# Two input chunks side by side, bias tiles and residual spread over one transfer queue, in a two-layer encoder trunk

## Chip, cores and metric

One core of one Trainium2 chip. The metric is the device time of one execution in microseconds (us). TensorE (PE) multiplies; VectorE (DVE) and ScalarE (ACT) prepare operands and do the elementwise work; GpSimd (POOL) and SyncE (SP) issue transfers, POOL with a little arithmetic. Each engine runs its own instructions in the order of a list that is fixed when the kernel is built; engines wait for each other through semaphores.

## The reference, cut

S = 256 tokens of width D = 2048, two layers. Only layer 0's attention and the bias table matter here.

```python
h = rms_norm(x, norm_attn[i])
proj = h @ w_in_a[j]                       # 2048 x 5120
q, k, v, q_m = jnp.split(proj, [MIX_WIDTH, 2 * MIX_WIDTH, 3 * MIX_WIDTH], axis=-1)   # MIX_WIDTH = 1536
q = rms_norm(q.reshape(B, S, N_HEADS, 2, DIFF_QK_DIM), a_q_norm[j])    # k alike; 12 heads
...
bias = rel_bias_lookup(rel_bias, positions[:, None, :] - pb[:, :, None])   # 32 buckets x 12 heads
s = s + jnp.transpose(bias, (0, 3, 1, 2))[:, :, None].astype(jnp.float32)
p = jax.nn.softmax(s, axis=-1)
a = p[:, :, 0] - lam * p[:, :, 1]
...
x = x + heads @ w_out[i]
h = rms_norm(x, norm_mlp[i])
x = x + jnp.square(jax.nn.relu(h @ w_up[i])) @ w_down[i]
```

## The kernel before

**Weights.** Every weight matrix is cut into chunks of 512 output columns, and a chunk of the input projection into 8 *pieces* of 128x1024 f32 (512 KB: two blocks of 128 rows of the matrix). `fetch` (L171) issues a piece's transfer on SP (L183), casts it on ACT to a rounded `hi` (L184) and subtracts on DVE to get the rest, `lo` (L185). `chunk_tok` (L264) runs 12 matmuls of 128x512 for each piece into two PSUM banks called mm: per block of rows and half of the tokens hi by x (L276), lo by x (L277), hi by the rest of x (L278). raw, hi and lo have four buffers each; `piece` keeps two pieces fetched ahead. Chunks 6 to 8 of the input projection are values, 0 to 2 queries, 3 to 5 keys. The order is 6, 0, 3, 7, 1, 4 and so on; pieces are counted here in that order over chunks, so chunk 6 is pieces 0 to 7, chunk 0 pieces 8 to 15, chunk 3 pieces 16 to 23, chunk 7 pieces 24 to 31 and chunk 1 pieces 32 to 39.

**The start.** Chunk 6 runs while the input arrives. Its pieces come in halves (256 KB); ahead of each half `first` (L732) loads x tiles on ACT's queue (L724) and splits one of 16 blocks of x on ACT and DVE (L200, L201). The residual `xt` is loaded in four parts of 512 KB on SP (L730); the parts stand behind the latest weight transfer (`tc.issue_after`).

**Tasks.** Everything else is cut into tasks, and `tick` (L138), called after each piece, runs the next step of the first ready task; that sets where the step's instructions come in the program, and a scheduler then sets the order on each engine by its own estimate of times. The 8 tasks `rows_done` build the bias: `bias_hot(i)` loads 4 blocks of 32x2048 buckets, issued by POOL (L560), and compares them with each partition's number (L562, DVE); `bias_rows(i)` looks the bias up by 48 small matmuls (L571, *rows* below) into two banks called aux and copies these, the first on DVE, the second on ACT (L572). `norm_T` squares a finished q or k chunk (L324), sums (L326), takes the root (L109 to L114), scales (L331) and transposes (L339); `row_stats` and `chunk_sq` do the like for x. `diff_head` does a head's scores (12 matmuls, L386), adds the bias and takes the maximum (L392, DVE), negates it (L394) and takes the exponent (L395, ACT), later the values.

**Lanes.** The transfers that SP and ACT issue take eight completion semaphores in turn; one is issued only when the transfer eight before it has landed.

Of the kernel before, what the change touches and what calls it, by code (L numbers as in the profile page):

```python
# [31 lines left out]
BW = 14  # L32
# [14 lines left out]
def trunk(ctx: ExitStack, tc: tile.TileContext, xin, xtok, memin, pos, rel, gcol, rows,  # L47
# [113 lines left out]
    for layer, (name, chunks) in enumerate((("a", (6, 0, 3, 7, 1, 4, 8, 2, 5, 9)), ("b", (3, 4, 0, 1, 2, 5)))):  # L161
        plan_chunks(name, chunks)
        plan_chunks(f"mem{layer}", range(2))
        plan_chunks(f"out{layer}", range(4))
        plan_chunks(f"up{layer}", range(16))
        plan_down(f"down{layer}")
# [4 lines left out]
    def fetch(parts=1, lead=None):  # L171

        name, c, j = plan.popleft()
        src = weights[name][c, j]
# [3 lines left out]
        n = 1024 // parts  # L178
        for i in range(parts):
            s = slice(i * n, (i + 1) * n)  # L180
            if lead is not None:
                lead(i)
            behind[0] = nc.sync.dma_start(raw[:, s], src[:, s])  # L183
            nc.scalar.copy(hi[:, s], raw[:, s])  # L184
            nc.vector.tensor_tensor(lo[:, s], raw[:, s], as32(hi)[:, s], op=ALU.subtract)  # L185
        ready.append(((name, c, j), hi, lo))

    def piece(name, c, j, lead=None):

        if lead is not None:  # L190
            fetch(2, lead)
        else:
            while plan and len(ready) <= AHEAD:
                fetch()
        key, hi, lo = ready.popleft()
        assert key == (name, c, j), (key, name, c, j)
        return hi, lo
# [66 lines left out]
    def chunk_tok(w, c, X2, before=None, lead=None, steps=1):  # L264
        ps = [bank("mm") for _ in range(2)]
        for j in range(8):
            if before is not None:
                before(j)
            hi, lo = piece(w, c, j, lead and (lambda i: lead(2 * j + i)))
            for kk in range(2):  # L270
                for t in range(2):
                    k = 2 * j + kk
                    ws = slice(kk * 512, kk * 512 + 512)
                    xh = X2[k][:, 0, t * P:(t + 1) * P]
                    xl = X2[k][:, 1, t * P:(t + 1) * P]
                    nc.tensor.matmul(ps[t], lhsT=xh, rhs=hi[:, ws], start=(k == 0), stop=False)  # L276
                    nc.tensor.matmul(ps[t], lhsT=xh, rhs=lo[:, ws], start=False, stop=False)  # L277
                    nc.tensor.matmul(ps[t], lhsT=xl, rhs=hi[:, ws], start=False, stop=(k == KT - 1))  # L278
            tick(steps)
        return ps  # L280

# [274 lines left out]
    def bias_hot(i):  # L556
        oh = blk([P, 8, S], BF16)
        hot = oh.rearrange("p r q -> p (r q)")
        for g in range(4):
            nc.gpsimd.dma_start(hot[32 * g:32 * g + 32, :],  # L560
                                bkt[g:g + 1, i * 2048:(i + 1) * 2048].broadcast_to([32, 2048]))
# [184 lines left out]
    rows_done = [Task([lambda i=i: bias_hot(i), lambda i=i: bias_rows(i, bias)], [prep], wait=BW) for i in range(8)]  # L746
# [103 lines left out]
```

## Time and profile before

| | us |
|---|---|
| three runs | 2148.4, 2149.2, 2148.91; median 2148.91 |
| the profiled execution | 2150.42 |
| its span on the core | 2148.6 |
| PE busy in the span | 2137.6 |

The profiled execution's own time is 1.8 us over its span and 1.5 us over the median of the runs. PE has some work in 99% of the span; the start of a matmul to the start of the next one tells more than the busy time, since matmuls overlap. The granted clock is 1.00 throughout, the 2.4 GHz level.

### The profile page before, as it was taken

What the parts mean: (1) busy time and instruction counts of PE and PEld (TensorE: products, weight loads), DVE (VectorE), ACT (ScalarE), POOL (GpSimd) and SP (SyncE); (2) the same over time, 40 slices, a digit from 0 to 9 for tenths busy, and PEclk for the clock granted to TensorE, in tenths of its full rate; (3) what the DMA queues carried; (4) which work ended last, traced back from release to release, by engine and by line L of the source; (5) the groups of instructions that cost most, each with busy time, mean ns of one, the idle gap of its engine ahead of it and who ended that gap; (6) DMA issues with size and microseconds to landing.
All of it is one profiled execution on the core that took longest, in us unless ns stands there. A gap on an engine that the chain in (4) does not pass through costs nothing.

```text
span 2148.6 us, 29416 instructions
## 1 busy us (share of the span) xinstructions
PE 2137.6 (99%) x11116; PEld 1806.4 (84%) x11116; DVE 1315.6 (61%) x2067; ACT 1083.6 (50%) x1740; POOL 35.7 (2%) x61
## 2 busy tenths in 40 slices
PE   9999999999999999999999999999999999999999
PEld 7877878888888888888888888888888888888887
DVE  7667786565555555566556677655555556556554
ACT  6456675454444445555545566554444444544443
POOL 1200020000000000000000000000000000000000
PEclk9999999999999999999999999999999999999999
DMA  8865565666666666666656656566666666666654
GB/s 292 237 209 154 157 195 153 187 183 189 185 194 188 191 186 193 193 195 235 198 194 192 181 167 178 155 183 183 185 195 188 192 189 185 196 196 212 192 193 148
DMA packets 114959, 409.24 MB, mean 190 GB/s; under 512 B 13568, under 2 KB 14336, under 8 KB 114560
## 3 DMA queue, kind: packets, MB, share of 16 engines
q1 hardware_dynamic: 111840, 401.01, 60.9%
q0 software_dynamic: 1536, 4.20, 0.8%
q10 hardware_dynamic: 1440, 2.15, 0.3%
q8 instruction: 87, 1.43, 0.3%
q14 instruction: 56, 0.46, 0.1%
HBM read 401.93 MB, written 5.37 MB: 190 GB/s over the span
## 4 chain that ended last, share of the span: by engine, by line
PE 97%; DMA 1%; DVE 1%; ACT 1%; issue 0%; SPq 0%; POOL 0%; ACTq 0%; DVEq 0%; POOLq 0%
PE mm L289 11%; PE aux L289 11%; PE mm L276 9%; PE mm L277 9%; PE mm L278 9%; PE mm L293 6%; PE aux L293 6%; PE mm L680 5%; PE mm L679 5%; PE mm L678 5%; PE aux L679 5%; PE aux L680 5%; PE aux L678 5%; DMA raw<-in_w_a 1%; PE aux L368 1%; PE aux L339 1%
## 5 line engine op out<-in xcount | busy, mean ns | idle before, releaser
L185 DVE TENSOR_TENSOR lo<-raw,hi 128x1024 fp32r<-128x1024 f32 (+1 forms) x744 | 892.7, 1214 | 747.7 <-ACT hi L184 747.3
L184 ACT CAST hi<-raw 128x1024 fp32r<-128x1024 f32 (+1 forms) x744 | 764.3, 1044 | 815.2 <-PE aux L289 194.1
L276 PE MATMUL mm<-hi,x 128*128 128x512 f32 x704 | 281.3, 401 | 2.0 <-ACT hi L184 2.0
L277 PE MATMUL mm<-lo,x 128*128 128x512 f32 x704 | 276.3, 392 | 2.1 <-DVE lo L185 2.1
L278 PE MATMUL mm<-hi,x 128*128 128x512 f32 x704 | 275.9, 392 | 0.0
L289 PE MATMUL mm<-x,hi 128*128 128x512 f32 x1024 | 247.4, 391 | 0.0
L289 PE MATMUL aux<-x,hi 128*128 128x512 f32 x1024 | 246.9, 391 | 0.0
L289 PEld LDWEIGHTS mm<-x,hi 128*128 128x128 f32 x1024 | 188.2, 188 | 36.8 <-DVE xt L642 0.5
L289 PEld LDWEIGHTS aux<-x,hi 128*128 128x128 f32 x1024 | 188.2, 188 | 36.4
L679 PE MATMUL aux<-lo,h 128*128 128x512 f32 x512 | 199.5, 390 | 0.5 <-DVE lo L185 0.5
L680 PE MATMUL aux<-hi,h 128*128 128x512 f32 x512 | 199.2, 389 | 0.0
L678 PE MATMUL aux<-hi,h 128*128 128x512 f32 x512 | 199.2, 389 | 0.0
L678 PE MATMUL mm<-hi,h 128*128 128x512 f32 x512 | 199.2, 389 | 0.0
L679 PE MATMUL mm<-lo,h 128*128 128x512 f32 x512 | 199.2, 389 | 0.0
L680 PE MATMUL mm<-hi,h 128*128 128x512 f32 x512 | 199.2, 389 | 0.0
L276 PEld LDWEIGHTS mm<-hi,x 128*128 128x128 f32 x704 | 132.2, 188 | 29.1 <-ACT hi L184 3.3
L277 PEld LDWEIGHTS mm<-lo,x 128*128 128x128 f32 x704 | 132.6, 188 | 28.2 <-DVE lo L185 4.2
L278 PEld LDWEIGHTS mm<-hi,x 128*128 128x128 f32 x704 | 132.2, 188 | 27.9 <-DVE x L201 0.2
L293 PEld LDWEIGHTS mm<-x,lo 128*128 128x128 f32 x1024 | 131.4, 191 | 4.8
L293 PEld LDWEIGHTS aux<-x,lo 128*128 128x128 f32 x1024 | 131.3, 191 | 5.0
L293 PE MATMUL mm<-x,lo 128*128 128x256 f32 x1024 | 133.3, 283 | 0.0
L293 PE MATMUL aux<-x,lo 128*128 128x256 f32 x1024 | 132.8, 283 | 0.0
(166 smaller groups left out, 2114.8 us busy)
## 6 DMA issues: line engine op xcount, KB each, us to landing
raw<-in_w_up SPq DMA_DIRECT2D x256, 512.0 KB, 3.9
raw<-in_w_down SPq DMA_DIRECT2D x256, 512.0 KB, 4.2
raw<-in_w_a SPq DMA_DIRECT2D x72, 512.0 KB, 4.0
raw<-in_w_out SPq DMA_DIRECT2D x64, 512.0 KB, 3.6
raw<-in_w_b SPq DMA_DIRECT2D x48, 512.0 KB, 3.7
raw<-in_w_mem SPq DMA_DIRECT2D x32, 512.0 KB, 3.8
raw<-in_w_a SPq DMA_DIRECT2D x16, 256.0 KB, 5.7
blk<-bkt POOLq DMA_DIRECT2D x32, 128.0 KB, 8.8
```

The source lines that it names most:

```text
L184: nc.scalar.copy(hi[:, s], raw[:, s])
L185: nc.vector.tensor_tensor(lo[:, s], raw[:, s], as32(hi)[:, s], op=ALU.subtract)
L276: nc.tensor.matmul(ps[t], lhsT=xh, rhs=hi[:, ws], start=(k == 0), stop=False)
L277: nc.tensor.matmul(ps[t], lhsT=xh, rhs=lo[:, ws], start=False, stop=False)
L278: nc.tensor.matmul(ps[t], lhsT=xl, rhs=hi[:, ws], start=False, stop=(k == KT - 1))
L289: nc.tensor.matmul(ps[o], lhsT=hi[:, cols(k % 2, o)], rhs=x2.rearrange("p a s -> p (a s)"), start=(k == 0), stop=(k == 2 * nj - 1))
L293: nc.tensor.matmul(ps[o][:, 256:512], lhsT=lo[:, cols(k % 2, o)], rhs=x2[:, 0, :], start=False, stop=False)
L339: nc.tensor.transpose(out=pt[:, h * P:(h + 1) * P], in_=qn[t][:, h * P:(h + 1) * P], identity=ident)
L368: nc.tensor.transpose(out=pt[:, kt * S + qt * P:kt * S + (qt + 1) * P], in_=p_of(qt)[:, kt * P:(kt + 1) * P], identity=ident)
L678: nc.tensor.matmul(ps[n][t], lhsT=xh, rhs=hi[:, ws], start=(k == 0), stop=False)
L679: nc.tensor.matmul(ps[n][t], lhsT=xh, rhs=lo[:, ws], start=False, stop=False)
L680: nc.tensor.matmul(ps[n][t], lhsT=xl, rhs=hi[:, ws], start=False, stop=(k == 4 * KT - 1))
```

## The change

- Chunks 6 and 0 run together (`chunk_pair`): for each of 8 steps both chunks' pieces are fetched, x is split once, and 24 matmuls run, chunk 6 into mm banks and chunk 0 into aux banks. Only step 0's pieces come in halves. The program calls `tick` twice after a step.
- The x loads go to SP's queue, ahead of the weights that need them.
- The residual comes in eight parts of 256 KB, six of them in the steps.
- The bucket tiles are loaded by SP instead of POOL, behind the latest weight transfer, and `rows_done[i]` may start at tick 16 + 2i instead of 14.
- Statistics of x and the values of chunk 6 move to behind the pair (`start_stats`), and the squares of chunk 0 behind them.

The line numbers of the changed kernel: weight transfer, cast, subtraction L174 to L176, chunk matmuls L272 to L274, x loads L744 and L758, residual L750, bucket load L583, comparison L584, rows L593, copies L594, squares L346, sums L348, root L109 to L114, scaling L353, scores L408, L414, L416, L417.

```diff
-BW = 14
+BW = 16
...
+    plan.extend(("a", c, j) for j in range(8) for c in (6, 0))
...
+    def chunk_pair(w, ca, cb, X2, lead, before):
+        pa = [bank("mm") for _ in range(2)]
+        pb = [bank("aux") for _ in range(2)]
+        for j in range(8):
+            if j == 0:
+                fetch(2, lead)
+            else:
+                before(j)
+            two = [(pa, *piece(w, ca, j)), (pb, *piece(w, cb, j))] if j else [...]
+            for kk in range(2):
+                for ps, hi, lo in two:
+                    mms_tok(ps, 2 * j + kk, hi, lo, X2)
+            tick()
+            tick()
...
     def bias_hot(i):
-        for g in range(4):
-            nc.gpsimd.dma_start(hot[32 * g:32 * g + 32, :],
-                                bkt[g:g + 1, i * 2048:(i + 1) * 2048].broadcast_to([32, 2048]))
+        with tc.issue_after(behind[0].ins):
+            for g in range(4):
+                nc.sync.dma_start(hot[32 * g:32 * g + 32, :], bkt[g:g + 1, i * 2048:(i + 1) * 2048].broadcast_to([32, 2048]))
...
+    def next_x(j):
+        if j == 1:
+            load_x(1)
+        load_x(j + 1)
+        take_x(2 * j)
+        take_x(2 * j + 1)
+        if j > 1:
+            load_residual(j - 2)
...
-    rows_done = [Task([lambda i=i: bias_hot(i), lambda i=i: bias_rows(i, bias)], [prep], wait=BW) for i in range(8)]
+    rows_done = [Task([lambda i=i: bias_hot(i), lambda i=i: bias_rows(i, bias)], [prep], wait=BW + 2 * i) for i in range(8)]
...
+    pv, pq = chunk_pair("a", 6, 0, X2, first_x, next_x)
...
+    stats = Task([lambda: (load_residual(6), load_residual(7))] + [lambda c=c: chunk_sq(c) for c in range(4)] + [start_stats],
+                 gap=1, front=True)
+    qT, qd = norm_T(pq, st0, 8, gs[:, 0:1], lambda: None)
+    qd.after.append(stats)
```

How this moves instructions is seen in the order of the built kernels.

SP's queue at the start before holds half pieces (raw) only, with the x tiles on ACT's queue; xt is the residual, rw, tab and t1k are small tables:

```order
L183 DMA raw_113<-in_w_a 128x512 x2
L183 DMA raw_147<-in_w_a 128x512 x2
L183 DMA raw_176<-in_w_a 128x512 x2
L183 DMA raw_205<-in_w_a 128x512 x2
L589 DMA rw<-in_rows 128x268
L541 DMA tab<-in_rel 32x12
L183 DMA raw_247<-in_w_a 128x512 x2
L730 DMA xt<-in_xtok 128x2x512
```

Now it holds the x tiles (xs) too, and two pieces for each step:

```order
L758 DMA xs_121<-in_xin 128x256
L174 DMA raw_115<-in_w_a 128x512
L174 DMA raw_118<-in_w_a 128x512
L758 DMA xs_121<-in_xin 128x256
L174 DMA raw_115<-in_w_a 128x512
L174 DMA raw_118<-in_w_a 128x512
L744 DMA xs_166<-in_xin 128x512
L744 DMA xs_168<-in_xin 128x512
L174 DMA raw_176<-in_w_a 128x1024
L174 DMA raw_182<-in_w_a 128x1024
```

The x loads moved from ACT's queue to SP's, ahead of the weights.

DVE before, in chunk 3: blk_602 is the bucket tile whose rows stand before piece 19, with aux_751 the first of its banks; lo_805, lo_875 and lo_945 belong to pieces 21, 22 and 23:

```order
L331 TENSOR_TENSOR t2k_635<-mm_376,sm_617 128x512
L562 TENSOR_SCALAR blk_602<-blk_602,itf 128x2048
L572 COPY big_110<-aux_681 128x12x4x8
L185 TENSOR_TENSOR lo_805<-raw_803,hi_804 128x1024
L572 COPY big_110<-aux_751 128x12x4x8
L185 TENSOR_TENSOR lo_875<-raw_873,hi_874 128x1024
L562 TENSOR_SCALAR blk_608<-blk_608,itf 128x2048
L572 COPY big_110<-aux_821 128x12x4x8
L185 TENSOR_TENSOR lo_945<-raw_943,hi_944 128x1024
```

DVE now, in the same chunk: blk_603 and blk_705 are the bucket tiles whose rows stand before pieces 20 and 22, aux_733 and aux_840 their first banks; lo_611, lo_685, lo_713 and lo_787 belong to pieces 20, 21, 22 and 23:

```order
L353 TENSOR_TENSOR t2k_909<-aux_113,sm_893 128x512
L353 TENSOR_TENSOR t2k_911<-aux_114,sm_893 128x512
L584 TENSOR_SCALAR blk_603<-blk_603,itf 128x2048
L594 COPY big_110<-aux_733 128x12x4x8
L176 TENSOR_TENSOR lo_611<-raw_609,hi_610 128x1024
L176 TENSOR_TENSOR lo_685<-raw_683,hi_684 128x1024
L584 TENSOR_SCALAR blk_705<-blk_705,itf 128x2048
L594 COPY big_110<-aux_840 128x12x4x8
L176 TENSOR_TENSOR lo_713<-raw_711,hi_712 128x1024
L176 TENSOR_TENSOR lo_787<-raw_785,hi_786 128x1024
L348 TENSOR_REDUCE sm_939<-t2k_941 128x8
L584 TENSOR_SCALAR blk_816<-blk_816,itf 128x2048
```

Before, a copy of the rows ahead of piece 19 stands between the lo of pieces 21 and 22; now the copy of the rows ahead of piece 22 stands before the lo of piece 22 itself, and the comparison of the tile for piece 24 behind a sum of chunk 3's squares.

PE now, at piece 22 (its hi is hi_712): the last of the 48 rows, then the piece's first matmuls:

```order
L593 MATMUL aux_866<-tab_453,blk_705 128x48
L272 MATMUL mm_559<-hi_712,x_464 128x512
L272 MATMUL mm_560<-hi_712,x_464 128x512
L273 MATMUL mm_559<-lo_713,x_464 128x512
L274 MATMUL mm_559<-hi_712,x_464 128x512
```

Two matmuls with hi stand between the rows and the first that needs lo. The rows stand before pieces 18 (partly 19), 20, 22, 24, 26, 28, 30 and 32 now, and before pieces 18, 19, 20, 21 (towards its end), 25, 26, 27 and 31 in the kernel before.

DVE now, ahead of piece 36: its lo, lo_1442, stands behind seven of the L414 (ISA with two outputs) of the first two heads, whose scores, with the third head's, stand on PE in one row of 36 matmuls ahead of the piece:

```order
L414 ISA t2k_1556,sm_1539<-aux_1542,big_110 128x256
L414 ISA sm_1539 128x1
L416 TENSOR_SCALAR sm_1491<-sm_1490 128x1
L414 ISA t2k_1556,sm_1539<-aux_1543,big_110 128x256
L414 ISA sm_1539 128x1
L416 TENSOR_SCALAR sm_1540<-sm_1539 128x1
L414 ISA t2k_1563,sm_1539<-aux_1542,big_110 128x256
L414 ISA sm_1539 128x1
L176 TENSOR_TENSOR lo_1442<-raw_1440,hi_1441 128x1024
```

Before, three heads' scores stand one head ahead of each of pieces 33, 34 and 35. From about piece 70 on, the two orders are the same.

## Rows read from the trace of the kernel before

**Rows 1.** The page's first part: busy time, share of the span and instructions of each engine.

```profile
PE 2137.6 (99%) x11116; PEld 1806.4 (84%) x11116; DVE 1315.6 (61%) x2067; ACT 1083.6 (50%) x1740; POOL 35.7 (2%) x61
```

**Rows 2.** Busy time by stretches of 10 us from the start: engines' busy us (instructions), then the granted clock, the DMA engines' busy share and GB/s.

```profile
0.00:10.00 10.00, 8.27 (x43) 6.95 (x44) 2.98 (x11) 3.45 (x6) 1.14 (x10) 1.00 0.77 264
10.00:20.00 10.00, 8.84 (x37) 6.36 (x36) 6.97 (x16) 5.80 (x13) 0.00 (x0) 1.00 0.99 318
20.00:30.00 10.00, 7.78 (x32) 5.43 (x31) 7.67 (x16) 7.67 (x16) 1.19 (x2) 1.00 0.85 262
```

**Rows 3.** Timeline of PE from the first matmul of chunk 6 (6.17) over chunk 0's first (34.53) to chunk 3's first (56.29): start, duration, then line, operation and, in brackets, the idle time before and what ended it. Some matmul records are missing from the trace.

```profile
6.17 0.50 PE L276 MATMUL mm<-hi,x 128*128 128x512 f32 x1
...
8.57 0.74 PE L276 MATMUL mm<-hi,x 128*128 128x512 f32 x2 [0.67 <-ACT hi L184]
...
15.41 0.50 PE L277 MATMUL mm<-lo,x 128*128 128x512 f32 x1 [0.61 <-DVE lo L185]
15.75 0.40 PE L278 MATMUL mm<-hi,x 128*128 128x512 f32 x1
...
21.45 0.73 PE L276 MATMUL mm<-hi,x 128*128 128x512 f32 x2 [0.76 <-ACT hi L184]
...
26.67 0.50 PE L277 MATMUL mm<-lo,x 128*128 128x512 f32 x1 [1.46 <-DVE lo L185]
...
34.53 0.39 PE L276 MATMUL mm<-hi,x 128*128 128x512 f32 x1
...
56.29 0.39 PE L276 MATMUL mm<-hi,x 128*128 128x512 f32 x1
```

**Rows 4.** Timeline of ACT around 20 us; ACTq is the issue of a transfer.

```profile
20.00 0.34 ACTq L724 DMA_DIRECT2D xs<-in_xin  x1
20.38 0.51 ACT L200 ACTIVATE x<-xs,gc 128x256 fp32r<-128x256 f32 x1 [4.21 <-DMA xt<-in_xtok]
```

**Rows 5.** Timeline of PE in chunk 3 at the rows of two bucket tiles.

```profile
61.74 1.38 PE L571 MATMUL aux<-tab,blk 128*128 128x48 bf16 x48
62.96 0.48 PE L276 MATMUL mm<-hi,x 128*128 128x512 f32 x1
63.28 0.40 PE L277 MATMUL mm<-lo,x 128*128 128x512 f32 x1
63.51 0.39 PE L278 MATMUL mm<-hi,x 128*128 128x512 f32 x1
...
69.83 1.38 PE L571 MATMUL aux<-tab,blk 128*128 128x48 bf16 x48
```

**Rows 6.** Timeline of DVE from the end of chunk 0 into chunk 3.

```profile
56.45 0.69 DVE L326 TENSOR_REDUCE sm<-t2k 128x8 f32<-128x512 f32 x1 [0.36 <-ACT t2k L324]
57.05 0.74 DVE L562 TENSOR_SCALAR blk<-blk,itf 128x2048 bf16<-128x2048 bf16 x1
...
59.57 0.22 DVE L327 TENSOR_SCALAR sm<-sm,st 128x8 f32<-128x8 f32 x1
...
62.64 0.17 DVE L112 TENSOR_TENSOR sm<-sm 128x16 f32<-128x16 f32 x1
...
63.26 1.29 DVE L331 TENSOR_TENSOR t2k<-mm,sm 128x512 f32<-128x512 f32 x2
64.46 0.75 DVE L562 TENSOR_SCALAR blk<-blk,itf 128x2048 bf16<-128x2048 bf16 x1
65.12 0.55 DVE L572 COPY big<-aux 128x384 f32<-128x384 f32 x1
65.59 1.22 DVE L185 TENSOR_TENSOR lo<-raw,hi 128x1024 fp32r<-128x1024 f32 x1
...
70.65 0.56 DVE L572 COPY big<-aux 128x384 f32<-128x384 f32 x1 [1.00 <-PE aux L571]
71.22 1.23 DVE L185 TENSOR_TENSOR lo<-raw,hi 128x1024 fp32r<-128x1024 f32 x1
```

**Rows 7.** Timeline of ACT in chunk 3: a cast and the two steps of a root.

```profile
60.41 1.05 ACT L184 CAST hi<-raw 128x1024 fp32r<-128x1024 f32 x1 [2.38 <-DMA raw<-in_w_a]
61.37 0.21 ACT L109 ACTIVATE sm<-sm 128x16 f32<-128x16 f32 x1
61.61 0.22 ACT L110 ACTIVATE sm<-sm 128x16 f32<-128x16 f32 x1
```

**Rows 8.** Timeline of PE, DVE and ACT around the scores of a head (three answers, one for each engine).

```profile
118.91 0.97 PE L386 MATMUL aux<-blk,blk 64*128 64x256 f32 x12
...
119.92 0.42 DVE L392 CUSTOM_DVE_ANT_0 t2k<-aux,big 128x256 f32<-128x256 f32 x1 [0.79 <-PE aux L386]
...
121.08 0.42 DVE L392 CUSTOM_DVE_ANT_0 t2k<-aux,big 128x256 f32<-128x256 f32 x1
...
121.49 1.22 DVE L185 TENSOR_TENSOR lo<-raw,hi 128x1024 fp32r<-128x1024 f32 x1
...
118.23 0.51 ACT L395 ACTIVATE t2k<-t2k,sm 128x256 f32<-128x256 f32 x1 [2.05 <-DVE sm L394]
...
118.74 0.49 ACT L395 ACTIVATE t2k<-t2k,sm 128x256 f32<-128x256 f32 x1
```

**Rows 9.** The page's last part: transfers by line, count, KB of each, median us from issue to landing.

```profile
raw<-in_w_a SPq DMA_DIRECT2D x72, 512.0 KB, 4.0
...
blk<-bkt POOLq DMA_DIRECT2D x32, 128.0 KB, 8.8
```

More of the change, by code (lines that the diff above doesn't have):

```diff
@@ L159, in plan_down @@
         plan.extend((name, c, j) for h in range(2) for j in range(32) for c in (2 * h, 2 * h + 1))
[L161 removed]
+    plan.extend(("a", c, j) for j in range(8) for c in (6, 0))
+    for layer, (name, chunks) in enumerate((("a", (3, 7, 1, 4, 8, 2, 5, 9)), ("b", (3, 4, 0, 1, 2, 5)))):
         plan_chunks(name, chunks)
@@ L169, in trunk, with fetch_part, new_piece @@
     behind = [None]
-    def fetch(parts=1, lead=None):
-        name, c, j = plan.popleft()
-        src = weights[name][c, j]
+    def fetch_part(key, raw, hi, lo, s):
+        name, c, j = key
+        behind[0] = nc.sync.dma_start(raw[:, s], weights[name][c, j][:, s])
+        nc.scalar.copy(hi[:, s], raw[:, s])
+        nc.vector.tensor_tensor(lo[:, s], raw[:, s], as32(hi)[:, s], op=ALU.subtract)
+    def new_piece():
         raw = wp.tile([P, 1024], F32, tag="raw", name=nm("raw"))
@@ L177, in fetch, with piece @@
         lo = wp.tile([P, 1024], F32R, tag="lo", name=nm("lo"))
[L178 to L181, printed above, removed]
-                lead(i)
[L183 to L194, printed above, removed]
+        return plan.popleft(), raw, hi, lo
+    def fetch(n=1, lead=None):
+        new = [new_piece() for _ in range(n)]
+        for i in range(2 if lead else 1):
+            if lead:
+                lead(i)
+            for p in new:
+                fetch_part(*p, slice(i * 512, i * 512 + 512) if lead else slice(0, 1024))
+        ready.extend((p[0], p[2], p[3]) for p in new)
+    def piece(name, c, j):
+        while plan and len(ready) <= AHEAD:
+            fetch()
         key, hi, lo = ready.popleft()
@@ L262, in to_features, with mms_tok, chunk_tok @@
         return Task([lambda: two(0), lambda: two(1)], wait=1, gap=1)
-    def chunk_tok(w, c, X2, before=None, lead=None, steps=1):
+    def mms_tok(ps, k, hi, lo, X2):
+        ws = slice((k % 2) * 512, (k % 2) * 512 + 512)
+        for t in range(2):
+            xh = X2[k][:, 0, t * P:(t + 1) * P]
+            xl = X2[k][:, 1, t * P:(t + 1) * P]
+            nc.tensor.matmul(ps[t], lhsT=xh, rhs=hi[:, ws], start=(k == 0), stop=False)
+            nc.tensor.matmul(ps[t], lhsT=xh, rhs=lo[:, ws], start=False, stop=False)
+            nc.tensor.matmul(ps[t], lhsT=xl, rhs=hi[:, ws], start=False, stop=(k == KT - 1))
+    def chunk_tok(w, c, X2, before=None, steps=1):
         ps = [bank("mm") for _ in range(2)]
@@ L268, in chunk_tok @@
                 before(j)
-            hi, lo = piece(w, c, j, lead and (lambda i: lead(2 * j + i)))
+            hi, lo = piece(w, c, j)
             for kk in range(2):
[L271 to L278, printed above, removed]
+                mms_tok(ps, 2 * j + kk, hi, lo, X2)
             tick(steps)
         return ps
+    def chunk_pair(w, ca, cb, X2, lead, before):
[6 more added lines that the diff above has]
+                before(j)
+            two = [(pa, *piece(w, ca, j)), (pb, *piece(w, cb, j))] if j else [(pa, *ready.popleft()[1:]), (pb, *ready.popleft()[1:])]
+            for kk in range(2):
+                for ps, hi, lo in two:
+                    mms_tok(ps, 2 * j + kk, hi, lo, X2)
+            tick()
+            tick()
+        return pa, pb
     def chunk_out(w, c, nj, x2_of, tag, steps=1):
```

51 lines of the change are left out of this document (22 added, 29 removed).

## The prediction

> **What bounds the kernel now.** The page's first part comes first: PE is busy 2137.6 us [rows 1], 99% of a span of 2148.6, so time can only come from the 11.0 us in which it has nothing, or go by adding to them. The stretches of 10 us show where they lie: PE works 8.27, 8.84 and 7.78 of the first three [rows 2], so 5.1 of the 11.0 us fall into the first 30 us, at the full clock. The timeline of PE is then read from start to start, because a matmul's end is modelled: chunk 6 goes from 6.17 to 34.53, 28.36 us, and chunk 0 behind it from 34.53 to 56.29, 21.76 us for the same 96 matmuls [rows 3]. Chunk 6 loses 6.60 us. In brackets stand its waits, for hi and lo in turn, with 1.46 us the longest. On ACT a wait of 4.21 us ends at 20.38 [rows 4], for a transfer of the residual: the x load issued at 20.00 stood behind a lane which that transfer held. Chunk 3 is read next, because the change moves its order: there PE goes from matmul to rows to matmul without a gap [rows 5].
>
> **Part 1: the pair.** A step of the pair is 24 matmuls, 2 x 21.76 / 8 = 5.44 us, and needs one step of x, where before a piece of 2.72 us needed it. ACT's work in a step is two casts of 1.05 [rows 7] and two x of 0.51 [rows 4], 3.1 us of 5.44. A step's bytes are two pieces (1.05 MB), x and residual (0.26 each), 1.57 MB; at the 318 GB/s that 10 to 20 us reached [rows 2] that is 4.9 us of 5.44. So both fit, with little to spare for the transfers. The tightest is step 1: by it 2.9 MB must be there (two steps of weights, three x tiles); the first 10 us moved 2.64 MB [rows 2], so the last piece lands near 10.8, its hi is there at 11.9 and PE wants it at 6.17 + 5.44 + 6 matmuls = 13.0. I let one wait stay, as long as the one of 0.76 [rows 3], and its restart: after a wait the second matmul comes 0.34 us behind the first (15.41 to 15.75 [rows 3]) where 0.23 is usual (63.28 to 63.51 [rows 5]). That makes 1.0 us with rounding; the ends are 0 and, if the bytes still bind, 4. Gain: 6.60 - 1.0 = **5.6 us**, at most 6.6, since the first matmul needs x and weights as before. What was hidden behind chunk 0 before, the bias steps on DVE, now lies in the pair; 3.4 us of a step's 5.44 would be DVE's own splitting if x took what it takes ACT (2 x 1.22 + 2 x 0.51), so 2 us of each step are left for it.
>
> The row of 0.99 for the transfers' share from 10 to 20 us [rows 2] says that the engines behind the queues were full there, whichever queue issued. The Trainium skill, page "DMA: Bandwidth & Descriptors", section "Issuing engines are not separate DMA queues", says that transfers started by different engines run on the same 16 engines, and that several starters save only the time to start. By that the move of x from ACT's queue to SP's would give nothing, and only the halved need for x would; by the wait of 4.21 us it gives the lane as well.
>
> **Part 2: rows and copies.** Here the order decides. Let T be the start of the 48 rows of a tile. The next matmul starts at T + 1.22, the next 0.32 later, the next 0.23 later [rows 5]. In the changed order two matmuls with hi follow the rows, so PE wants lo at T + 1.77. On DVE that lo now stands behind the copy of the rows' first bank. A copy that waited for the rows began 0.82 us after they did (69.83 [rows 5], 70.65 [rows 6]), the lo behind it 0.57 later, and a lo takes 1.23 [rows 6]: T + 2.62. PE waits 0.85, and 0.11 for the restart: **0.96 us each time**. Before, the same copy stood behind the lo of two pieces further on, and the wait of 1.00 us for the rows [rows 6] cost PE nothing. The ends are 0 (lo not late) and 2.6 (if the copy cost its whole chain). By the places of the rows:
> - Pieces 22, 26 and 28: 0.96 each, 2.9.
> - Piece 19: its lo stands behind the first copy and the small sums of x, whose root passes ACT ahead of its hi. Taking T as the start of piece 18, the copy begins at 1.3 (the first bank's rows are cut by two matmuls, 0.82 + 0.45) and takes 0.47 (65.12 to 65.59 [rows 6]); three small steps of 0.2 and the root's first step of 0.21 [rows 7] bring it to 2.6, the cast (1.05) to 3.6, lo to 4.8. PE wants it at 1.22 + 2.72 + 0.55 = 4.5: 0.4 with the restart.
> - Piece 20: the comparison of its tile stands on DVE behind all the statistics of chunk 0. From 4.8: two sums of 0.60 (56.45 to 57.05), three small steps of a root (0.2 each, as 62.64 to 63.26), two of 0.2 for the means [all rows 6] give 7.0; the root on ACT 0.45 [rows 7], 0.62 for its steps on DVE and 1.20 for the two scalings (63.26 to 64.46), and 0.66 for the comparison (64.46 to 65.12 [rows 6]) give 9.9. PE is there at 2.72 + 1.22 + 2.72 + 0.4 = 7.1. It waits 2.8, then 0.96 for lo: 3.8.
> - Piece 24: the comparison stands behind the first sum of chunk 3's squares. At the end of chunk 0 (56.29 [rows 3]) such a sum began at 56.45 and a comparison behind it ended at 57.79 [rows 6], 1.5 us after PE had passed. So 1.5 + 0.96 = 2.5.
> - Pieces 30 and 32: transposes stand behind the rows and cover most; 0.7 for both (ends 0 and 1.9).
> - Piece 36: three heads' scores in a row. The first L392 starts 1.01 after the scores, the fourth ends 2.58 after them (118.91, 121.49 [rows 8]), then three more of 0.39 each end at 3.7. The cast of the piece stands on ACT behind two exponents of 0.5 [rows 8], which start near 1.8: 1.8 + 1.0 + 1.05 = 3.85, lo at 5.1. Without waits PE wants it at 3 x 0.97 + 0.55 = 3.5. Loss 1.7 with the restart. Before, the heads come one to a piece, with lo pieces ahead.
>
> Sum: 0.4 + 3.8 + 2.9 + 2.5 + 0.7 + 1.7 = **12.0 us lost**. Uncertain are above all pieces 20, 24 and 36, which rest on where other chains end; without all of the three but their 0.96 the sum is 6.9. Both orders are alike from piece 70 on, and the work between has slack; I put that at nothing.
>
> **Moved queues.** Issue by SP instead of POOL saves POOL's starting of 32 transfers, which nothing waited for on PE. The tiles' four transfers now stand ahead of each second pair of pieces on SP and hold four of the eight lanes; the pieces are some three ahead (8 us) and take 4.0 us to land, a tile's block 8.8 in the crowd of before [rows 9]. I put it at nothing, since PE's own waits lengthen the pair of pieces from 6.7 to 7.6 us; the price if wrong is rival D.
>
> **Net**: 12.0 - 5.6 = +6.4 us. The profiled execution (2150.42) would go to 2156.8, its span to 2155.0; the runs' median of 2148.91 to **2155.3 us**. A measurement of this kernel tells about 0.2%, 4.3 us, from no change.
>
> **Rivals.**
> - **B, a draw.** The chain at pieces 20 and 24 ends before PE gets there, and the scores find their banks free: only the waits of 0.96 stay, six to eight of them with piece 19, 5.5 to 8 us, against 5.6 to 6.6. Net -1 to +2.4: about 2149.5. It decides if DVE's chain behind the first copy takes 7 us instead of 9.9. Against it: every step of that chain has a row. For it: it needs DVE and ACT to be as late as I assume throughout.
> - **C, faster.** lo is there in time at every piece. Place: DVE at pieces 20 to 32; it decides when lo comes 0.85 us sooner after the rows, which the durations do not allow unless DVE starts a lo whose inputs are ready while the copy ahead of it still waits. Then the pair's gain is left, 5.6 to 6.6: 2142.3 to 2143.3, plus what piece 36 costs. Against it: the copy of 70.65 waited and the lo came directly behind [rows 6], though that row alone does not prove an order, as a cast ended close by.
> - **D, transfers late.** A ring of eight lanes at 8.8 us per transfer [rows 9] issues six transfers in 6.6 us, and a pair of pieces with its tile needs just these six in 6.7. If the weights share that latency, each tile adds some us from piece 18 on: about 5 more in all, 2160 and above. For it: transfers ran at a share of 0.99 [rows 2]. Against it: without the POOL queue's crowding the block of 128 KB should land near the 4.0 of a piece.
> - **E, the change does not do what it says.** The start stays bound by bytes: the loss of 6.60 falls by 2 or 3 only, since a step has 0.5 us to spare at 318 GB/s and needs 1.57 MB each time. Net +9 to +10: about 2158.5.
>
> The Trainium skill, page "PSUM — Partial Sum Buffer", section "Engine vs sequencer instructions", calls the queues of ScalarE and VectorE strict FIFO and says that matmuls start in program order. By that rule C's way is shut; the rows above agree but do not show it by themselves.
>
> **How the numbers follow.** Forecast (A, 2153.2 to 2159) 0.52, since each term follows from an order that is fixed and from durations with rows. B 0.24, because three terms of 1.5 us or more rest on chains. C 0.11, E 0.07, D 0.06. Slower by over 0.2% (above 2153.2) is A, E and D, 0.65; same is B, 0.24; faster (below 2144.6) is C, 0.11. The range from 2146.5 to 2160.5 leaves out C, most of D and the ends.
>
> **What would show it.** Part 1: from the first chunk matmul to the first of chunk 3, 43.52 + 1 us, with chunk 3 starting near 50.7. Part 2: PE waits of about 0.9 us for lo (released by L176) behind the rows of pieces 22, 26 and 28, and waits of 1.5 to 3 us at the rows themselves of pieces 20 and 24, released by L584; one of about 1.7 us at the third head's scores and piece 36. Wrong would be: no wait of PE behind the rows (C), waits of hi for raw in chunk 3 (D), or a chunk 3 that starts after 53 us (E).

## The result, and the profile after

The changed kernel took a median of 2157.62 us (2156.15 to 2159.84, 6 runs), the kernel before 2148.65 beside it (2147.55 to 2150.32, 6 runs). The ratio is 1.0042, with an interval of 1.0029 to 1.0055: slower, by about 9 us. The profiled execution took 2157.89 us, its span 2155.8. The forecast was 2155.3, slower.

The first reading is the page's busy line (columns as in [rows 1]).

```profile
PE 2140.8 (99%) x11116; PEld 1810.7 (84%) x11116; DVE 1315.1 (61%) x2061; ACT 1081.8 (50%) x1734; POOL 17.7 (1%) x29
```

PE has the same matmuls and 15.0 us in which it did nothing, where there were 11.0. It was also busy 3.2 us longer: 1.3 of these are the warm-up matmuls (6.59 us against 5.26), and a stretch at a lower clock adds 1.4, worked out below. Where that stretch is, the stretches tell (columns as in [rows 2]; the last three are places that the readings below come to).

```profile
0.00:10.00 10.00, 8.95 (x43) 8.50 (x44) 4.52 (x13) 5.51 (x9) 1.13 (x10) 1.00 0.75 238
10.00:20.00 10.00, 9.92 (x44) 7.86 (x43) 8.43 (x16) 7.17 (x10) 0.00 (x0) 1.00 0.92 345
20.00:30.00 10.00, 10.00 (x46) 8.29 (x45) 7.78 (x13) 7.42 (x14) 1.19 (x2) 1.00 0.96 360
60.00:70.00 10.00, 7.17 (x85) 5.21 (x85) 7.78 (x17) 5.00 (x11) 0.00 (x0) 1.00 0.85 221
130.00:133.00 3.00, 2.11 (x14) 1.47 (x14) 2.86 (x17) 3.00 (x8) 0.00 (x0) 1.00 0.25 100
134.00:136.00 2.00, 2.00 (x6) 1.58 (x5) 2.00 (x7) 2.00 (x7) 0.00 (x0) 0.50 0.75 248
```

The idle time of the first 30 us is down from 5.1 to 1.1 [rows 2], and the DMA engines moved 345 and 360 GB/s where 318 and 262 stood. The loss lies behind: PE works 7.17 of the 10 us from 60, 2.11 of the 3 us from 130, and at 134 to 136 its granted clock is 0.50, the lower of the two levels (1.2 GHz).

PE's timeline, from the warm-up matmuls over the first of the pair (7.40) and of chunk 3 (51.48) to the rows of pieces 20 and 22, the rows of piece 24, the scores ahead of piece 36, and the first matmul of piece 56:

```profile
1.05 6.59 PE L99 MATMUL aux<-ones 128*128 128x128 f32 x32 [1.05 <-DVE ones L96]
7.40 0.48 PE L272 MATMUL mm<-hi,x 128*128 128x512 f32 x1
...
51.48 0.39 PE L272 MATMUL mm<-hi,x 128*128 128x512 f32 x1
...
66.41 1.38 PE L593 MATMUL aux<-tab,blk 128*128 128x48 bf16 x48 [2.20 <-DVE blk L584]
67.64 0.71 PE L272 MATMUL mm<-hi,x 128*128 128x512 f32 x2
68.97 0.50 PE L273 MATMUL mm<-lo,x 128*128 128x512 f32 x1 [0.62 <-DVE lo L176]
...
74.07 1.38 PE L593 MATMUL aux<-tab,blk 128*128 128x48 bf16 x48
75.29 0.71 PE L272 MATMUL mm<-hi,x 128*128 128x512 f32 x2
76.62 0.50 PE L273 MATMUL mm<-lo,x 128*128 128x512 f32 x1 [0.62 <-DVE lo L176]
...
83.31 1.38 PE L593 MATMUL aux<-tab,blk 128*128 128x48 bf16 x48 [1.39 <-DVE blk L584]
85.89 0.50 PE L273 MATMUL mm<-lo,x 128*128 128x512 f32 x1 [0.65 <-DVE lo L176]
...
130.08 1.38 PE L408 MATMUL aux<-blk,blk 64*128 64x256 f32 x12 [0.56 <-DVE sm L414]
131.81 0.73 PE L272 MATMUL mm<-hi,x 128*128 128x512 f32 x2 [0.34 <-ACT hi L175]
133.06 0.74 PE L273 MATMUL mm<-lo,x 128*128 128x512 f32 x1 [0.53 <-DVE sm L416]
...
134.03 0.63 PE L273 MATMUL mm<-lo,x 128*128 128x512 f32 x1
134.46 0.63 PE L274 MATMUL mm<-hi,x 128*128 128x512 f32 x1
...
201.94 0.39 PE L272 MATMUL mm<-hi,x 128*128 128x512 f32 x1
```

The row of 133.06 names L416 as what ended the wait; the lo that it needs ran on DVE from 131.78 to 133.01. From such starts the span falls into four parts. The kernel before reached piece 56 at 194.78.

| us | to the first chunk matmul | pair (before: chunks 6, 0) | chunk 3 to piece 56 | from there to the end |
|---|---|---|---|---|
| before | 6.17 | 50.12 | 138.49 | 1953.8 |
| after | 7.40 | 44.08 | 150.46 | 1953.9 |
| difference | +1.2 | -6.0 | +12.0 | +0.1 |

So the pair gains what its waits had cost, 6.0 of 6.60 us, a slower warm-up takes 1.2 of it away, and the third part, where the order is new, loses twice the gain. These are two executions; how much of the 6.0 belongs to them and not to the kernels is taken up where the prediction is judged.

How one wait comes about is read on DVE, around the rows of pieces 20 and 22:

```profile
65.61 0.74 DVE L584 TENSOR_SCALAR blk<-blk,itf 128x2048 bf16<-128x2048 bf16 x1
67.23 0.56 DVE L594 COPY big<-aux 128x384 f32<-128x384 f32 x1 [0.87 <-PE aux L593]
67.70 1.22 DVE L176 TENSOR_TENSOR lo<-raw,hi 128x1024 fp32r<-128x1024 f32 x1
...
74.88 0.56 DVE L594 COPY big<-aux 128x384 f32<-128x384 f32 x1 [3.70 <-PE aux L593]
75.36 1.21 DVE L176 TENSOR_TENSOR lo<-raw,hi 128x1024 fp32r<-128x1024 f32 x1
```

ACT's record of the same stretch has the cast that the lo of 75.36 needs:

```profile
69.73 1.05 ACT L175 CAST hi<-raw 128x1024 fp32r<-128x1024 f32 x1
```

That hi was there at 70.8. With four buffers for lo, the one that it needs was last read by piece 18's matmuls, of which the last began at 60.50. DVE had nothing to do for 3.70 us and still didn't start the lo: the copy stood ahead of it, waiting for rows that PE began at 74.07. PE then wanted lo 1.77 us after the rows' start, at 75.84, and got it at 76.62. The Trainium skill, page "PSUM — Partial Sum Buffer", section "Engine vs sequencer instructions", calls VectorE's queue strict FIFO; these rows agree, with 3.70 us beside it. Rival C needed the opposite.

The page's last part (columns as in [rows 9]) has the moved transfers on SP's queue, the tiles' blocks landing sooner than the 8.8 us of before:

```profile
raw<-in_w_a SPq DMA_DIRECT2D x78, 512.0 KB, 4.3
...
blk<-bkt SPq DMA_DIRECT2D x32, 128.0 KB, 6.7
```

### The profile page after: what moved, and what is told of

Same layout as the page of the kernel before. It is cut to its first block, busy times and chain, and to the rows that moved or that the text cites. A ratio compares the mean times of both kernels' runs of the same rounds, so it can differ in the third digit from the quotient of the medians.

```text
span 2155.8 us, 29373 instructions
## 1 busy us (share of the span) xinstructions
PE 2140.8 (99%) x11116; PEld 1810.7 (84%) x11116; DVE 1315.1 (61%) x2061; ACT 1081.8 (50%) x1734; POOL 17.7 (1%) x29
## 4 chain that ended last, share of the span: by engine, by line
PE 94%; DMA 3%; DVE 2%; ACT 1%; issue 1%; SPq 0%; POOL 0%; DVEq 0%; POOLq 0%; ACTq 0%
PE mm L311 11%; PE aux L311 11%; PE mm L273 8%; PE mm L274 8%; PE mm L272 8%; PE mm L315 6%; PE aux L315 6%; PE mm L701 5%; PE mm L700 5%; PE mm L702 5%; PE aux L701 5%; PE aux L702 5%; PE aux L700 5%; DMA raw<-in_w_a 2%; PE aux L390 1%; DVE lo L176 1%
## 5 line engine op out<-in xcount | busy, mean ns | idle before, releaser
L176 DVE TENSOR_TENSOR lo<-raw,hi 128x1024 fp32r<-128x1024 f32 (+1 forms) x738 | 891.5, 1222 | 730.7 <-ACT hi L175 729.7
L273 PE MATMUL mm<-lo,x 128*128 128x512 f32 x672 | 264.9, 394 | 3.7 <-DVE lo L176 3.1
L272 PE MATMUL mm<-hi,x 128*128 128x512 f32 x672 | 268.1, 402 | 0.5 <-ACT hi L175 0.3
L274 PE MATMUL mm<-hi,x 128*128 128x512 f32 x672 | 264.1, 393 | 0.0
L273 PEld LDWEIGHTS mm<-lo,x 128*128 128x128 f32 x672 | 127.2, 189 | 30.4 <-DVE lo L176 7.3
L274 PEld LDWEIGHTS mm<-hi,x 128*128 128x128 f32 x672 | 126.7, 189 | 26.4
L272 PEld LDWEIGHTS mm<-hi,x 128*128 128x128 f32 x672 | 126.0, 189 | 24.8 <-ACT hi L175 0.9
(173 smaller groups left out, 2155.3 us busy)
```

## The experiments

Each is compared with the kernel before in runs on the same chip. "Stages" are the first three columns of the table above, from the profiled execution. The theory throughout is the prediction's: the loss is the order on DVE, where copies of the rows stand ahead of a piece's lo, and comparisons behind the statistics.

**lo_first: the copies behind the next lo.** The changed kernel, with the copies queued after the latest lo that has been fetched.

```diff
-        nc.vector.tensor_tensor(lo[:, s], ...)
+        last_lo[0] = nc.vector.tensor_tensor(lo[:, s], ...)
...
+            with tc.issue_after(last_lo[0].ins):
                 (nc.scalar.copy if qt else nc.vector.tensor_copy)(...)
```

> The changed kernel with one thing altered: the copies of the bias rows are queued behind the newest lo on VectorE and behind nothing else new; TensorE's order stays, except that the three heads' scores no longer stand in one row but ahead of three pieces. Theory (TensorE waits because lo stands behind a copy that itself waits for the rows): the five waits of about 0.9 us behind the rows of pieces 20 to 28 go (4.5 us), and the loss of about 3.5 us at piece 36 with its slow clock goes; the waits at the rows of pieces 20 and 24 (2.4 and 1.6 us, released by the comparison) stay. Time about 8 us below the changed kernel, near 2149.5, the same as before within 2 us. Rival (VectorE is simply short of time there, whatever the order): the waits move to other places and the time stays within 3 us of the changed kernel's 2157.6.

Median 2151.29 us against 2149.8, ratio 1.0008 [0.9999, 1.0017]. Stages 6.49, 47.16, 144.44: the third is 6.0 shorter than in the changed kernel. PE at the rows of piece 20 and at the first matmuls of piece 22:

```profile
67.36 1.38 PE L594 MATMUL aux<-tab,blk 128*128 128x48 bf16 x48 [1.10 <-DVE blk L585]
...
75.36 0.71 PE L273 MATMUL mm<-hi,x 128*128 128x512 f32 x2
75.91 0.39 PE L274 MATMUL mm<-lo,x 128*128 128x512 f32 x1
```

The matmul with lo follows 0.55 us behind the first with hi, without a wait. Waits for the comparisons (L585 here) stay, 1.10 us at piece 20 and 1.39 at piece 24 (2.20 and 1.39 in the changed kernel). So the lo term is shown, and the time comes within 2 us of the kernel before, as the theory had it. One thing went along that was not asked for: the scores of the heads now stand one head to a piece, so that piece 36's loss went too. Five lo losses of 0.9, 3.5 at piece 36 and 1.1 of the wait at piece 20 make 9.1; a new wait of 1.3 (for values, at 141.28) and one of 0.2 (lo at piece 24) leave 7.6. Seen were 6.0 in this profile; 1.6 us are not accounted for.

**tiles_on_pool: the tiles from POOL's queue again.** The changed kernel, its bucket tiles loaded by POOL, without the order behind a weight transfer.

```diff
-        with tc.issue_after(behind[0].ins):
-                nc.sync.dma_start(hot[...], bkt[...])
+                nc.gpsimd.dma_start(hot[...], bkt[...])
```

> The changed kernel with only the bucket tiles' transfers issued by GpSimd again, no longer behind the weight transfers on SyncE; starts at tick 16 + 2i as in the changed kernel. The built order then has lo two pieces ahead of each copy and the scores apart. Theory: all of the 12 us lost behind the pair are a matter of that order, so they go, and the pair's gain stays: 2157.6 - 12 = 2145.6, about 3 us below before. Rival (the tiles crowd the transfers and weights come late when GpSimd issues them): waits for raw in chunk 3, 2150 or more. Rival (the pair's gain is eaten by the later statistics anyway): 2149 to 2152.

2160.98 us, ratio 1.0048 [1.0035, 1.0060]; stages 6.19, 50.45, 149.43. The theory's number fell, the rival was right: the pair took 6.4 us more than in the changed kernel and chunk 3 no less. By the ratios' intervals the two kernels are not told apart. Waits of 45 to 90 us (what waited, us in all, times, longest), then the transfers issued in 40 to 85 us:

```profile
ACT hi L175 <- DMA raw<-in_w_a: 19.8, 10, 3.2
```

```profile
raw<-in_w_a SPq DMA_DIRECT2D x13, 512.0 KB, 13.0
blk<-bkt POOLq DMA_DIRECT2D x32, 128.0 KB, 8.6
```

All 32 tile transfers fall into that stretch, where the changed kernel had 24, and a weight piece takes 13.0 us to land where it took 7.6. The kernel before, with all 32 there too but no pair, had 9.7. The crowd stands at the end of the pair: in 40 to 55 us the three are 13.5, 8.7 and 6.1, while in 50 to 90 tiles_on_pool has 7.6. In 45 to 90 ACT waits 19.8 us for weights, in the changed kernel 3.8. The page "DMA: Bandwidth & Descriptors" of the Trainium skill, section "Issuing engines are not separate DMA queues", says that a second starter saves only starting time. The landing times agree that the 16 engines are shared. What the move to SP brings besides is an order: a tile waits behind a weight transfer. Whether order or queue does it, no run separates, since none held POOL behind the weights.

**rows_alone: the second part of the change alone.** The kernel before, its tiles on SP behind the latest weight transfer, `wait=BW + 2 * i` with `BW = 16`.

```diff
-BW = 14
+BW = 16
...
+        with tc.issue_after(behind[0].ins):
-                nc.gpsimd.dma_start(hot[...], bkt[...])
+                nc.sync.dma_start(hot[...], bkt[...])
...
-wait=BW)
+wait=BW + 2 * i)
```

> The kernel before with only the second part of the change: bucket tiles issued by SyncE behind the latest weight transfer, starts at tick 16 + 2i; input chunks one after the other as before. The built order has lo behind the copies at pieces 22, 24, 26, 28, 30 and 32, the comparison for piece 24 behind a sum, and three heads' scores in a row ahead of piece 36. Theory: this part loses by itself what it loses in the whole change, less the wait at piece 20: 0.9 x 3 + 2.5 + 0.7 + 3.5, about 9 to 10 us: 2158 to 2159. Rival (it loses only because the pair moved the statistics next to it): within 3 us of before.

2155.89 us, ratio 1.0027 [1.0018, 1.0036], some 6 us slower, less than expected. Stages 6.35, 48.16, 144.47. PE's waits:

```profile
82.03 1.38 PE L571 MATMUL aux<-tab,blk 128*128 128x48 bf16 x48 [1.39 <-DVE blk L562]
...
131.82 0.50 PE L277 MATMUL mm<-lo,x 128*128 128x512 f32 x1 [0.52 <-DVE lo L185]
```

The losses at pieces 24, 26, 28 and 36 are there without the pair, and no others: the rows from 62.67 to 78, those of piece 22 among them, stand without a wait, and the clock does not fall. From start to start these losses come to 6.2 us, and the third stage is 6.0 longer than in the kernel before. The long wait at piece 20 is thus the two parts' together: with the pair the statistics of x and the values of chunk 6 lie in chunk 3, ahead of that comparison.

**pair_alone: the first part alone.** The changed kernel with POOL's queue as in tiles_on_pool, `BW = 14` and `wait=BW`.

> The changed kernel without its bias part: bucket tiles issued by GpSimd and started at tick 14, as before; pair, x on SyncE and residual blocks as changed. The built order has lo two pieces ahead of the copies. Theory now (tiles that GpSimd issues in one go crowd the weights out when they meet the pair's heavier transfers, as in the kernel with the tiles on GpSimd): 2152 to 2160, with waits of TensorE for hi whose raw came late between 45 and 85 us, and 10 us or more from issue to landing of a weight. Rival (that crowd came from the later, spread start, not from GpSimd): the weights land in time, and the pair's gain shows: 2143 to 2147.

2161.92 us against 2149.04, ratio 1.0064 [1.0050, 1.0078]; stages 6.95, 47.84, 152.00. The weights land late, in 12.9 us in 40 to 85, as the theory said, but the time is above its range, and the wait that costs is not for hi. One wait of PE makes most of it, and its chain is read backwards from PE to DVE to ACT (three answers):

```profile
70.94 1.12 PE L593 MATMUL aux<-tab,blk 128*128 128x48 bf16 x24 [8.29 <-DVE big L594]
...
65.76 0.16 DVE L241 TENSOR_REDUCE sm<-ssq 128x2 f32<-128x8 f32 x1 [3.21 <-ACT t2k L237]
...
69.19 1.23 DVE L176 TENSOR_TENSOR lo<-raw,hi 128x1024 fp32r<-128x1024 f32 x1 [2.10 <-ACT hi L175]
70.33 0.55 DVE L594 COPY big<-aux 128x384 f32<-128x384 f32 x1
...
65.01 0.63 ACT L237 ACTIVATE t2k<-xt 128x512 f32<-128x512 f32 x1 [1.56 <-DMA xt<-in_xtok]
...
68.12 1.04 ACT L175 CAST hi<-raw 128x1024 fp32r<-128x1024 f32 x1 [1.75 <-DMA raw<-in_w_a]
```

The rows need a bank that the copy at 70.33 sets free. That copy stood behind a lo whose weights landed late, and that behind a sum of x's squares whose residual landed late. So the crowded transfers reach PE by way of DVE's order. The third stage is 13.5 us longer than in the kernel before: what the pair gains by itself (47.84 against 50.12) is lost several times over while the tiles still come all at once from POOL.

**tiles_on_pool_x_on_act: x from ACT's queue too.** As tiles_on_pool, with both x loads on `nc.scalar`.

> As the kernel with the tiles on GpSimd, but the x tiles of the pair are loaded on ScalarE's queue, as before the change. Theory of the lane (an x load on ScalarE's queue stands behind a lane that a residual transfer holds): the pair, 44.1 us from its first matmul to chunk 3's, becomes 2 to 5 us longer, with a wait of ScalarE for a residual transfer. Rival (which engine starts a transfer hardly matters; the halved need for x is what shortened the start): the pair stays within 0.7 us of 44.1 and the time within 1 us of the kernel with the tiles on GpSimd.

2153.97 us, ratio 1.0019 [1.0010, 1.0028]; stages 7.15, 47.50, 147.65. The pair did not get longer than the 50.45 of tiles_on_pool. As the tiles crowd both kernels, this says nothing on x in the changed one; the last run below asks again. The time is 7 us below that of tiles_on_pool, with intervals of the ratios that don't touch. Neither the theory nor the rival has that: here a weight piece lands in 10.2 us in 40 to 85 instead of 13.0, and why is open.

**changed_again: the changed kernel, one more profile.** No edit.

> The changed kernel once more, for a second profile. Theory: the waits behind the rows of pieces 20 to 28 (about 0.8 us each, 2.4 and 1.6 at the rows of 20 and 24) are the same to 0.1 us, since they follow from the order; what differs between executions is the start: the moment of the first chunk matmul (7.40 in the first profile), the length of the pair (44.1), and the granted clock at piece 36 (it fell to 0.50 in the first profile). Rival: the fall of the clock belongs to the order and comes again at the same place.

2156.62 us, span 2154.6; stages 6.71, 45.38, 149.32. PE at piece 20, and at the matmul behind the wait of piece 36:

```profile
67.02 2.10 PE L593 MATMUL aux<-tab,blk 128*128 128x48 bf16 x48 [2.24 <-DVE blk L584]
...
134.22 0.50 PE L273 MATMUL mm<-lo,x 128*128 128x512 f32 x1 [0.53 <-DVE sm L416]
```

Two stretches of it, behind each of the two waits:

```profile
69.00:70.00 1.00, 1.00 (x7) 0.48 (x3) 0.89 (x1) 0.84 (x2) 0.00 (x0) 0.50 0.06 25
133.00:135.00 2.00, 1.47 (x5) 0.93 (x6) 2.00 (x6) 2.00 (x6) 0.00 (x0) 1.00 0.01 2
```

The waits come back to within 0.04 us. The clock's fall does not: it comes behind piece 20 here and behind piece 36 there.

**lo_first_compare_first: comparisons ahead of the statistics too.** lo_first, with the comparison of a tile queued ahead of the sums of chunks 0 and 3 and of the statistics of x.

```diff
+        last_cmp[0] = nc.vector.tensor_scalar(hot, hot, ...)
...
+                if t == 0 and len(tabs) < 16 and last_cmp[0] is not None:
+                    with tc.issue_after(last_cmp[0].ins):
+                        red()
...
+        with tc.issue_after(last_cmp[0].ins):
             row_stats(st0)
```

> As lo_first, and the comparisons of the bucket tiles stand ahead of the statistics of x and of the sums for chunks 0 and 3 on VectorE. Theory (the two waits at the rows of pieces 20 and 24 come from comparisons that stand behind statistics): these 1.25 and 1.55 us go: 2148 to 2149, 2 to 3 us below lo_first's 2151.3. Rival (the statistics come later and their readers, the transposes and the scaled tiles, wait in their place): no change within 1.5 us.

2150.92 us against 2149.04, ratio 1.0008 [0.9999, 1.0017], the ratio of lo_first: by the times the rival. Stages 6.20, 45.59, 141.96. The waits of lo_first at the rows of pieces 20 and 24 are gone or short (0.42 is the longest), and others stand behind them, for hi and lo of a piece (PE):

```profile
87.63 0.73 PE L274 MATMUL mm<-hi,x 128*128 128x512 f32 x2 [0.66 <-ACT hi L177]
...
88.89 0.50 PE L275 MATMUL mm<-lo,x 128*128 128x512 f32 x1 [0.53 <-DVE lo L178]
```

So part of what is pushed back on DVE came due elsewhere. That it all did is not shown: in this profile the third stage is 2.5 us shorter than lo_first's, as the theory wanted. But the profiled execution, at 2148.97 us, is the fastest of eleven, while lo_first's, at 2153.5, is 2.2 above its median. The medians show no gain, and what the slower executions lose no trace shows.

**lo_first_no_spread: the tiles not spread.** lo_first with `BW = 14` and `wait=BW` for all tiles, still on SP behind weight transfers.

> As lo_first, but all bucket tiles may start at tick 14 as before the change, instead of 16 + 2i; issued by SyncE behind the latest weight transfer all the same. Theory (the spread is not what costs or gives; the place of lo is): waits of 1 us or less behind the rows, the scores end earlier: 2147 to 2150. Rival (tiles in a row on SyncE's queue make the weights behind them late): waits for raw of several us in chunk 3, 2152 or more.

2159.95 us, ratio 1.0054 [1.0041, 1.0066]; stages 6.63, 49.42, 149.71. This interval is clear of lo_first's. PE's longest wait, and the rows of ACT that lead to it:

```profile
88.29 1.22 PE L273 MATMUL mm<-hi,x 128*128 128x512 f32 x2 [3.11 <-ACT hi L176]
...
86.84 0.22 ACT L109 ACTIVATE sm<-sm 128x16 f32<-128x16 f32 x1 [1.02 <-DVE sm L350]
87.21 1.03 ACT L176 CAST hi<-raw 128x1024 fp32r<-128x1024 f32 x1
```

The cast that PE waits for stands on ACT behind the steps of a root, and these waited for DVE's sums over the chunk just finished. So the rival has the time, but not the way: ACT waited for raw 1.5 us at most in 52 to 100, and a weight piece landed in 7.8 us in 40 to 85, in lo_first in 9.3. The spread earns its place: without it the ratio is 0.0046 higher, about 10 us, though the copies stand behind lo. In this trace the loss is one of order again, now on ACT, with the granted clock at 0.50 from 88 to 94.

**lo_first_sums_last: a milder order.** As lo_first_compare_first, but the statistics of x stay where they were, and `BW = 15`.

> As lo_first, with the bias starts at tick 15 + 2i instead of 16 + 2i and, on VectorE, the comparisons ahead of the sums for chunks 0 and 3 (not ahead of the statistics of x). In the built order no lo and no comparison that TensorE needs next stands behind a chain of statistics, and the rows go 24 at a time ahead of pieces 19 to 26. Theory (all that the change loses behind the pair is a matter of places on VectorE): no wait over 1 us between the pair and piece 32, the pair's 4 to 5 us stay, 2145 to 2147.5, below before's 2149. Rival (the work moved behind the pair is too much for VectorE and ScalarE there, whatever the order): waits of 1 us and more somewhere between pieces 18 and 45, 2149 to 2152 as with lo_first.

2147.84 us (11 runs, 2146.64 to 2148.9) against 2149.49, ratio 0.9990 [0.9981, 0.9999]; stages 7.21, 45.05, 139.58. PE's rows at the two waits that are left:

```profile
62.17 0.78 PE L600 MATMUL aux<-tab,blk 128*128 128x48 bf16 x24 [0.26 <-DVE blk L591]
...
92.03 0.50 PE L275 MATMUL mm<-lo,x 128*128 128x512 f32 x1 [0.21 <-DVE lo L178]
```

With both orders mended, and the tiles started one tick earlier, the third stage is 10.9 us shorter than in the changed kernel, and the pair's gain comes out. How much the earlier tick has of it no run separates. It is the fastest of the kernels here, ahead of the kernel before by 0.1%, with an interval that only just leaves out 1; that is a little less than expected.

**lo_first_sums_last_x_on_act: x on ACT's queue, without the crowd.** The same with both x loads on `nc.scalar`.

> As lo_first_sums_last, but the x tiles of the pair are loaded on ScalarE's queue, as before the change; behind the pair the order is the same except for 24 rows that go one piece later. Theory of the lane: x comes late in some step because its load stands behind a full lane on ScalarE, which also holds up the casts; the pair is 2 to 5 us longer and the time too. Rival (the queue hardly matters; the halved need for x does): the pair's length and the time are within 1 us of lo_first_sums_last.

2149.05 us, ratio 0.9999 [0.9990, 1.0008]; stages 6.71, 48.18, 138.70. The pair took 3.1 us more, the whole 1.2 us more, between the two expectations. An x of ACT in the pair:

```profile
33.66 0.91 ACT L205 ACTIVATE x<-xs,gc 128x256 fp32r<-128x256 f32 x2 [1.85 <-DMA xs<-in_xin]
```

ACT waited for an x load there, with casts behind it in its queue. But the pair with unaltered instructions took 44.08, 45.38, 45.59 and 47.16 us in four executions (after, changed_again, lo_first_compare_first, lo_first), so 48.18 is not far enough from them to say that the queue did it. Open.

## Why the prediction was right, and where it was off

**The pair.** Predicted gain 5.6, seen 6.0 from matmul to matmul between the two profiled executions. In place of the one wait of 1.0 us, 0.56 are left over 43.52. That this came so near is partly luck: with the same order on DVE, ACT and SP the pair took 45.38, 45.59 and 47.16 us in changed_again, lo_first_compare_first and lo_first, 1.9 to 3.6 over 43.52. Chunks 6 and 0 one after the other, with the same order on DVE and ACT, took 48.16 in rows_alone instead of 50.12. So the gain lies between 1.0 and 6.0; an estimate from the means of these four and two lengths is 3.6, 2 less than forecast. The step "since the first matmul needs x and weights as before" left out the warm-up matmuls ahead of it. They took 6.59 us, not 5.26, in that execution, and 5.90 in changed_again, so the first stage varied by more than the term is worth. Rival E fell in the changed kernel: chunk 3 began at 51.48, and the transfers reached 360 GB/s. The byte estimate took 318 GB/s for a bound, and the changed kernel passed it.

**Rows and copies.** The sum was 12.0 and the stretch grew by 11.97; term by term it is less exact. Seen values are starts against the spacing that the matmuls have without a wait.

| term | predicted | seen |
|---|---|---|
| piece 19 | 0.4 | 0 |
| piece 20: comparison, then lo | 2.8 + 0.96 | 2.4 + 0.9 |
| pieces 22, 26, 28 | 2.9 | 2.7 |
| piece 24 | 2.5 | 2.5 |
| pieces 30, 32 | 0.7 | 0.4 |
| piece 36 | 1.7 | 3.5 |

The seen terms add up to 12.4, 0.4 over the stretch's 11.97. Piece 20's long chain was the boldest step and held: T of piece 18 was 56.92, and its comparison ended 9.4 us later instead of 9.9, with PE there 7.1 us later as worked out. Piece 36 is the term that was mis-sized. Its waits came to about 2.1 us, and then seven intervals between matmuls were 0.43 us instead of 0.23, 1.4 us more, at the granted clock of 0.50. The prediction had no term for the clock; that its other terms were a little high hid this, so that the sum of 12.0 meets the 11.97 partly by luck.

**Net.** Between the two profiled executions the spans went from 2148.6 to 2155.8, +7.2 where +6.4 was forecast: the pair 0.4 better, the first matmul 1.2 worse. The medians lie 9.0 apart, since the profiled execution before was 1.8 us above its median, and that after 0.3 above its own. The median of 2157.62 is 2.3 above the forecast. That is about what the pair's gain falls short by in the estimate above; whether it is the reason, no run shows.

**Moved queues.** "I put it at nothing" was right as a sum and wrong as a view. Against the kernel before, PE sees nothing of it; the weights land in 7.6 us in 40 to 85, where the kernel before had 9.7. But tiles_on_pool and pair_alone show that the pair leaves the transfers little room: there a weight piece takes 13.0 and 12.9 us to land in that stretch, ACT waits 19.8 and 17.4 us for weights, and the time is above that of lo_first, whose copies also stand behind lo, by 0.4% and more (1.0048 and 1.0064 against 1.0008). lo_first_no_spread loses about as much by another way, with weights that land in time. As far as these runs go, moving and spreading the tiles is what makes the pair's gain possible, and the order that came with it on DVE is what loses it. For that reason the parts don't add up: the pair alone costs 0.64%, the rows alone 0.27%, both 0.42%.

**Rivals.** B's condition was not met (the chain took 9.4 us, not 7). C fell by the 3.70 us in which DVE stood idle with a ready lo behind the copy, and by lo_first. D didn't occur in the changed kernel, where PE had no wait for hi from chunk 3 on before piece 36. A weight piece took 7.6 us to land in 40 to 85. The 4.0 that the prediction set against D is the median over the whole kernel [rows 9], 4.3 now; in that stretch the kernel before itself had 9.7. A tile's block landed in 6.7, not near 4.0. In tiles_on_pool, with 13.0 us, D occurred.

## What to carry to other kernels

Where an engine works its queue in order, place an instruction that waits for the bottleneck engine behind all that this engine will want next: here a copy in front of a lo cost 0.9 us each time, and moving it behind the lo gave that back. Two good parts can be needed together, and be judged wrongly alone; cost each part in the company of the other. Read a gain of a few us over several executions of both kernels: the pair alone varied by 3.1. A gain at the start of a kernel is kept only if the work that it displaces has somewhere to go that isn't ahead of an operand.

## What was not expected of the hardware

- The granted clock fell to 0.50 (1.2 GHz) behind different waits in two executions of one program: behind piece 36 in the first, behind piece 20 in the second, though the waits were alike (2.20 and 2.24 us at piece 20). Ahead of the fall in the first, PE had worked 2.11 of the 3 us from 130. In rows_alone it had worked 2.13 of the 3 us ahead of its piece 36, and the clock stayed. Its windows there:

```profile
129.00:132.00 3.00, 2.13 (x15) 1.49 (x16) 2.86 (x15) 3.00 (x8) 0.00 (x0) 1.00 0.06 22
132.00:134.00 2.00, 2.00 (x9) 1.62 (x10) 2.00 (x7) 2.00 (x6) 0.00 (x0) 1.00 0.57 117
```

  What decides, these rows don't tell; it stays open.
- The 32 warm-up matmuls took 5.26 us before, 6.59 after and 5.90 in changed_again, and moved the first chunk matmul from 6.17 to 7.40 and 6.71. Nothing of them was changed. The Trainium skill, page "TensorE: Matmul & The Clock Gate", section "What's actually happening", says that the point of the clock's rise differs from run to run of the same kernel. The matmuls' spacing agrees: 4 or 5 of them start in half a microsecond from 1.5 us until about 4.0 us before, 7.0 after and 5.5 in changed_again, and 6 or 7 from there. The granted clock in the profile does not show it; it reads 1.00 from the start in all three.
- The pair, with the same order of instructions, took 44.08, 45.38, 45.59 and 47.16 us in four executions, the last with PE waits of up to 0.76 us for lo. In 20 to 30 us of the first the transfers' share was 0.96. This stage varies by 3.1 us, half of what the pair gained between the two profiled executions.
